# Feed-forward parts of 8 chunks recut to 6, with fewer plain chunks and the operands' steps behind them

## The chip, the cores and the metric

The kernel runs on one core of a Trainium2 chip. The metric is the device time of one execution in microseconds (us), lower is better. TensorE (PE in the profile, its weight loads PEld) multiplies, VectorE (DVE) and GpSimd (POOL) work elementwise, ScalarE (ACT) copies, casts and evaluates functions, SyncE (SP) issues most DMAs.

## The reference

A decoder trunk of two layers on 512 tokens with 1024 features, all in float32. Layer 0 has a causal convolution module, layer 1 differential attention. Behind each comes the same feed-forward and a gated input embedding; the change concerns the feed-forward alone:

```python
D_FF = 2816
def swiglu(x, w_gate, w_up, w_down):
    return (jax.nn.silu(x @ w_gate) * (x @ w_up)) @ w_down
...
u = rms_norm(h, ffn_norm_g[i])
h = h + swiglu(u, ffn_w_gate[i], ffn_w_up[i], ffn_w_down[i])
gate = jax.nn.sigmoid(rms_norm(h, ple_norm_g[i]) @ ple_w_gate[i])
h = h + gate * (p[i] @ ple_w_proj[i])
```

## The kernel before

Features lie on the 128 partitions and tokens along the free axis, so h is eight tiles h[0] to h[7] of 128x512. For accuracy each product of two float32 matrices is three matmuls on rounded operands (`mm3`, L166 to L168): low weight by high input, high by high, high by low. Each weight tile is therefore split into whi (a rounding copy on ScalarE, L159) and wlo (a subtraction on VectorE, L161); the raw tiles have two buffers, whi and wlo four each.

The 2816 hidden features are 22 chunks of 128. They are computed in parts (`PARTS`, pairs of first chunk and count): each part computes its hidden chunks, and a down-projection (`linear`) then adds their share of the result to h. That projection takes eight output tiles m = 0 to 7, the first two of them together, with a weight tile, an accumulator in one of four PSUM banks (mm) and an addition into h on VectorE (L881) for each.

In the first part the chunks are plain. A chunk is a gate and an up product over all eight input tiles, matmuls of 512 columns. The norm's factors are not in the input but come later as rb, since their sum of squares is done beside the first chunk; VectorE multiplies them in (L869, L871), ScalarE applies silu, VectorE multiplies gate by up (L872), and the result is split into high (ScalarE, L874) and low (VectorE, L875) halves, the hidden chunk B0, B1 and so on.

In the other parts two chunks are taken together, and gate and up each become a unit (`Gate`, `Up`) that does the two-by-two block product with seven products in place of eight (a Strassen-like scheme). A product is four groups of three matmuls of 256 columns. For the units the input has to be there as seven combined operands (B11, B21, B22 and T1 to T4), each with high and low parts. `Operands.chunk(k, rb)` makes a quarter of them, for k = 0 to 3, from h and rb: nine instructions on VectorE (L667 twice, L674 to L677, L680, L682, L685) and three on ScalarE (L670, L672, L679), through the temporary tiles B6 and B7, which have one buffer each. These are "the operands' four steps"; `OPS_AT` names the plain chunks behind which they are written down.

The weights of a unit need sums as well: `Unit.prep`, steps 0 to 5, has four sums on POOL (L720, L721, L732, L733), and splits on ScalarE and VectorE (L710, L711; for the first unit of a part L726, L727; L736, L737). `run` interleaves the products of a unit with the preparation of the next one. Products p(4) and p(3) of a unit are done within the next unit; those of a part's last unit come last of all, and its last hidden chunks go through L794, L799, L801 and L802. The first unit of a part is loaded and prepared at m = 5, 6 and 7 of the down-projection ahead of it (`HOOKS`).

The order of instructions on each engine is not the order of the text: a planner places them by the readiness that it simulates, except where an order is written out. So a VectorE instruction can stand ahead of one that the text has earlier.

Of the kernel before, what the change touches and what calls it, by code (L numbers as in the profile page):

```python
# [23 lines left out]
NC = D // P  # L24
# [2 lines left out]
KW = 31  # L27
DFF = 2816
FC = DFF // P
PARTS = [(0, 6), (6, 8), (14, 8)]  # L30
EPS = 1e-6
LAMBDA_INIT = 0.8 - 0.6 * math.exp(-0.3 * 1)
NEG = -1.0e30
# [44 lines left out]
LT = 2  # L78
LA = 4
PACK = True  # L80
OPS_AT = (1, 2, 4, 5)
HOOKS = {5: (None,), 6: (1, 3), 7: (0, 2, 4, 5)}
HT = S // 2
E1 = True
GLO = 1
QKV = (("q", 0, (0, 0, 0, 0)), ("v", 0, (1, 1, 1, 2)), ("q", 1, (1, 1, 1, 2)), ("q", 2, (1, 1, 2, 1)), ("v", 1, (1, 1, 2, 2)), ("q", 3, (1, 1, 1, 1)))

PROJ1 = 16 + 2 + 8 + 2 * FC + 3 * NC + 8 + 4 * len(QKV)


@with_exitstack
def trunk(ctx, tc, xT, pT, wts, diag, dww, vec, rel, onehot, lamv, out):
# [54 lines left out]
    def weight(n=1024, pieces=1, between=(), eng=V, after=(None, None), home=None, parts=None, bufs=1):  # L147
        i = wnext[0]
        wnext[0] += 1
        raw = sb([P, 1024], *(home or ("wraw", 2)))  # L150
        hi = sb([P, 1024], *((parts[0], bufs) if parts else ("whi", 4)), F32R)
        lo = sb([P, 1024], *((parts[1], bufs) if parts else ("wlo", 4)), F32R)
        for k in range(pieces):
            cut = slice(k * n // pieces, (k + 1) * n // pieces)
            loaded[0] = nc.sync.dma_start(raw[:, cut], wts[i, :, cut])
            if k < len(between):
                between[k]()
            with tc.issue_after(after[1].ins) if after[1] else nullcontext():
                A.copy(hi[:, cut], raw[:, cut])  # L159
            with tc.issue_after(after[0].ins) if after[0] else nullcontext():  # L160
                eng.tensor_tensor(lo[:, cut], raw[:, cut], f(hi[:, cut]), ALU.subtract)  # L161
        return hi, lo
# [7 lines left out]
    def weight_in_h(i, c):  # L170

        raw = sb([P, 1024], "wraw", 2)
        nc.sync.dma_start(raw, wts[i])
        parts = [], []
        for k in range(2):
            cut = slice(k * S, (k + 1) * S)
            hi, lo = (sb([P, S], f"h{c + 2 * j + k}", 1, F32R) for j in range(2))
            A.copy(hi, raw[:, cut])
            V.tensor_tensor(lo, raw[:, cut], f(hi), ALU.subtract)
            parts[0].append(hi)  # L180
            parts[1].append(lo)
        return parts
# [622 lines left out]
    def ffn(norm, after, spare):  # L805
# [44 lines left out]
        us = None  # L850
        for at, (f0, n) in enumerate(PARTS):
            if us:
# [4 lines left out]
            for i in range(0 if us else n):  # L857
# [18 lines left out]
                hid.append((hl[:, 0], hl[:, 1]))  # L876
                if i in OPS_AT:
                    ops.chunk(OPS_AT.index(i), rb)

            def add(m, acc):  # L880
                V.tensor_tensor(h[m], acc, h[m], ALU.add)  # L881
                if at == len(PARTS) - 1:
                    after.chunk(m)

            hooks = {}
            if at < len(PARTS) - 1:
                n2 = PARTS[at + 1][1]
                now = wnext[0]
# [146 lines left out]
    def unit_end(pair, tb, q):  # L1035
        t = tp()
        for i in range(4):
            T.transpose(t[:, i * P : (i + 1) * P], q[:, i * P : (i + 1) * P], ident)  # L1038
        t4 = t.rearrange("p (h c t) -> p h c t", h=2, c=2)
        cut = slice(tb * P, (tb + 1) * P)  # L1040
        qs, ks, kl = qk[pair][0:2], qk[pair][2:4], qk[pair][4:6]

        qg, kg = col("q_g"), gains[:, 0:1]
        for c in range(2):
            own, other = HALVES[c], HALVES[1 - c]
            A.activation(qs[c][own, :, cut], t4[own, :, 0], AF.Copy, scale=qg[own])
            A.activation(ks[c][own, :, cut], t4[own, :, 1], AF.Copy, scale=kg[own])
            if KDUP == "A":
                A.activation(ks[c][other, :, cut], t4[own, :, 1], AF.Copy, scale=kg[own])
            else:  # L1050
                G.tensor_copy(ks[c][other, :, cut], f(ks[c][own, :, cut]))
        for c in range(2):
            own, other = HALVES[c], HALVES[1 - c]
            V.scalar_tensor_tensor(
                qs[c][other, :, cut], t4[own, :, 0], qg[own], f(qs[c][own, :, cut]), ALU.mult, ALU.subtract)
            V.scalar_tensor_tensor(
                kl[c][own, :, cut], t4[own, :, 1], kg[own], f(ks[c][own, :, cut]), ALU.mult, ALU.subtract)
# [122 lines left out]
    for what, at, pace in QKV:  # L1180
        ws = slab(GLO if at > 0 else 0)
        for tb in range(4):
# [12 lines left out]
            elif (what, at, tb) == ("q", 0, 2):  # L1195
                n = wnext[0]
                wnext[0] = PROJ1
                pw = [weight(parts=("B6", "B7"))]
# [6 lines left out]
            elif (what, at, tb) == ("q", 2, 1):  # L1205
                pw.append(weight_in_h(PROJ1 + 1, 0))
            elif (what, at, tb) == ("q", 2, 2):
                w_o1 = weight_in_h(PROJ1 + 3, 4)
            elif (what, at, tb) == ("q", 3, 1):
                wnext[0] = PROJ1 + 2  # L1210
                w_o0 = weight(parts=("B0", "B1"))
                wnext[0] = PROJ1 + 4
    unit_end(*waiting)
# [85 lines left out]
def _layout(a):  # L1299
# [12 lines left out]
    def ffn(i):  # L1312
        g, u = _stationary(a["ffn_w_gate"][i]), _stationary(a["ffn_w_up"][i])
        r = []
        for f0, n in PARTS:
            plain = n if f0 == 0 else 0
# [84 lines left out]
```

## Time and profile before

| | us |
|---|---|
| median of 3 runs | 1249.58 (1247.31 to 1250.39) |
| profiled execution | 1249.66 |
| its span, first to last instruction | 1247.6 |
| TensorE busy | 1236.4 |
| VectorE busy | 877.6 |
| ScalarE busy | 623.0 |
| POOL busy | 470.5 |

The granted clock of TensorE was 0.999 over the span. Matmuls overlap in time: each row shows a duration longer than the step from one start to the next, so the step is the pace. In the rows of the profile, tile names stand without buffer numbers: A is the plain input's split tiles (and the units' raw weights and sums), B the hidden chunks and the temporaries B6 and B7, C, wth and bias the combined operands, wraw, whi and wlo the weights, big and wk the work tiles.

### The profile page before, as it was taken

To read this page: it belongs to the slowest core of one execution; us is meant where nothing else is said; L and a number is where in the kernel's file an instruction comes from. 1 tells how busy PE (TensorE), PEld (TensorE's weight loads), DVE (VectorE), ACT (ScalarE), POOL (GpSimd) and SP (SyncE) were. 2 spreads that over 40 slices of the span, in tenths; PEclk is the share of its full clock that TensorE was granted. 3 is DMA by queue.
4 is the path that set the end of the run, shared out by engine and by line. 5 is a ranking of instruction groups with operands and counts; after the bars stand their busy time and mean duration, and the time that the engine had idled before them with its cause. 6 is when DMAs were issued, how large, how long until landed. Compare 5 with 4: busy or idle time off the path is not lost.

```text
span 1247.6 us, 18420 instructions
## 1 busy us (share of the span) xinstructions
PE 1236.4 (99%) x7080; PEld 1081.5 (87%) x7080; DVE 877.6 (70%) x1230; ACT 623.0 (50%) x1096; POOL 470.5 (38%) x355
## 2 busy tenths in 40 slices
PE   9999999999999999999999999999999999999998
PEld 7888788888998899888888888788889998999887
DVE  6998866985895478546676876646966885588535
ACT  5653464533553255334666877735434552455432
POOL 3763442024670365132346635041026640562220
PEclk9999999999999999999999999999999999999999
DMA  7566214324233322334432331142333333233321
GB/s 267 175 205 206 82 51 121 96 97 127 85 102 118 102 87 76 109 104 143 122 119 75 113 92 36 51 147 88 92 118 97 102 117 108 82 102 88 104 97 67
DMA packets 49154, 136.33 MB, mean 109 GB/s; under 512 B 5635, under 2 KB 10243, under 8 KB 49068
## 3 DMA queue, kind: packets, MB, share of 16 engines
q1 hardware_dynamic: 46944, 131.74, 33.7%
q10 hardware_dynamic: 2124, 3.43, 1.0%
q8 instruction: 55, 0.90, 0.3%
q14 instruction: 31, 0.25, 0.1%
HBM read 128.84 MB, written 6.31 MB: 108 GB/s over the span
## 4 chain that ended last, share of the span: by engine, by line
PE 88%; DVE 5%; issue 2%; DMA 1%; ACT 1%; SPq 0%; POOL 0%; DVEq 0%; ACTq 0%
PE mm L166 27%; PE mm L167 27%; PE mm L168 27%; PE mm L1117 1%; DVE sc L449 1%; DVE wlo L161 1%; PE sc L1085 1%; PE sc L1084 1%; PE tp L1104 1%; PE sc L398 1%; PE mm L398 1%; PE tp L1038 1%; PE mm L354 1%; PE tp L199 1%; DVE wlo L711 0%
## 5 line engine op out<-in xcount | busy, mean ns | idle before, releaser
L159 ACT CAST whi<-wraw 128x1024 fp32r<-128x1024 f32 (+2 forms) x145 | 145.6, 1013 | 220.2 <-PE mm L168 97.2
L161 DVE TENSOR_TENSOR wlo<-wraw,whi 128x1024 fp32r<-128x1024 f32 (+2 forms) x141 | 179.3, 1277 | 73.7 <-ACT whi L159 73.5
L166 PE MATMUL mm<-A,wlo 128*128 128x512 f32 (+1 forms) x568 | 222.5, 392 | 0.3 <-ACT A L206 0.2
L167 PE MATMUL mm<-A,whi 128*128 128x512 f32 (+1 forms) x568 | 219.8, 388 | 0.0
L168 PE MATMUL mm<-A,whi 128*128 128x512 f32 (+1 forms) x568 | 217.6, 389 | 0.0
L166 PE MATMUL mm<-B,wlo 128*128 128x512 f32 x352 | 137.9, 392 | 0.0
L167 PE MATMUL mm<-B,whi 128*128 128x512 f32 x352 | 137.8, 391 | 0.0
L168 PE MATMUL mm<-B,whi 128*128 128x512 f32 x352 | 136.2, 391 | 0.0
L229 POOL TENSOR_TENSOR acc<-acc,wk 128x512 f32<-128x512 f32 x35 | 58.3, 1665 | 194.5 <-ACT wk L228 193.9
L166 PEld LDWEIGHTS mm<-A,wlo 128*128 128x128 f32 x568 | 106.9, 188 | 23.6 <-issue 1.4
L167 PE MATMUL mm<-C,whi 128*128 128x256 f32 x448 | 127.0, 283 | 0.0
L168 PE MATMUL mm<-C,whi 128*128 128x256 f32 x448 | 127.0, 283 | 0.0
L166 PE MATMUL mm<-C,wlo 128*128 128x256 f32 x448 | 127.0, 283 | 0.0
L167 PEld LDWEIGHTS mm<-A,whi 128*128 128x128 f32 x568 | 107.0, 188 | 22.0 <-issue 1.0
L168 PEld LDWEIGHTS mm<-A,whi 128*128 128x128 f32 x568 | 106.6, 188 | 21.9 <-issue 0.5
L711 DVE TENSOR_TENSOR wlo<-A,whi 128x1024 fp32r<-128x1024 f32 x60 | 104.6, 1752 | 21.0 <-ACT whi L710 21.0
L710 ACT CAST whi<-A 128x1024 fp32r<-128x1024 f32 x60 | 62.9, 1048 | 56.6 <-PE mm L168 45.3
L720 POOL TENSOR_TENSOR A<-wraw 128x512 f32<-128x512 f32 x16 | 25.4, 1589 | 170.3 <-DMA wraw<-in_wts 156.1
L720 POOL TENSOR_TENSOR A<-A 128x512 f32<-128x512 f32 x16 | 25.3, 1581 | 161.9 <-DMA A<-in_wts 159.2
L167 PEld LDWEIGHTS mm<-C,whi 128*128 128x128 f32 x448 | 86.1, 192 | 0.2
L166 PEld LDWEIGHTS mm<-C,wlo 128*128 128x128 f32 x448 | 86.1, 192 | 0.2
L168 PEld LDWEIGHTS mm<-C,whi 128*128 128x128 f32 x448 | 86.1, 192 | 0.0
(309 smaller groups left out, 3030.6 us busy)
## 6 DMA issues: line engine op xcount, KB each, us to landing
wraw<-in_wts SPq DMA_DIRECT2D x161, 512.0 KB, 3.6
A<-in_wts SPq DMA_DIRECT2D x32, 512.0 KB, 3.6
wraw<-in_wts SPq DMA_DIRECT2D x16, 384.0 KB, 3.1
D<-in_diag SPq DMA_DIRECT2D x22, 256.0 KB, 4.7
C<-in_diag SPq DMA_DIRECT2D x16, 256.0 KB, 4.4
h<-in_xT SPq DMA_DIRECT2D x8, 256.0 KB, 5.2
rest<-h SPq DMA_DIRECT2D x8, 256.0 KB, 2.5
bias<-scr ACTq DMA_DIRECT2D x8, 256.0 KB, 3.7
```

Source lines behind the costliest of these rows:

```text
L159: A.copy(hi[:, cut], raw[:, cut])
L161: eng.tensor_tensor(lo[:, cut], raw[:, cut], f(hi[:, cut]), ALU.subtract)
L166: T.matmul(acc, al, bh, start=first, stop=False, **kw)
L167: T.matmul(acc, ah, bh, start=False, stop=False, **kw)
L168: return T.matmul(acc, ah, bl, start=False, stop=last, **kw)
L199: r = T.matmul(t[:, cut], src[:, cut], ones, start=first and b == 0, stop=last and b == 3)
L229: self.last = self.eng.tensor_tensor(self.acc, self.acc, sq, ALU.add)
L354: last_tap[0] = T.matmul(acc, dg[:, j % 4], ups[c][:, j : j + S], start=(j == 0), stop=(j == PE_TAPS[c] - 1))
L398: last_tap[0] = T.matmul(acc[:, g * P : (g + 1) * P], w, ups[c][:, g, LEAD - m : LEAD - m + P], start=(m == 0), stop=(m == LAGS - 1),)
L710: A.copy(hi, src)
L711: V.tensor_tensor(lo, src, f(hi), ALU.subtract)
L720: G.tensor_tensor(s[:, 0], r1[:, 0], r1[:, 1], ALU.add)
```

## The change

Three constants and a count:

```diff
-PARTS = [(0, 6), (6, 8), (14, 8)]
+PARTS = [(0, 4), (4, 6), (10, 6), (16, 6)]
...
-OPS_AT = (1, 2, 4, 5)
+OPS_AT = (0, 1, 2, 3)
...
-PROJ1 = 16 + 2 + 8 + 2 * FC + 3 * NC + 8 + 4 * len(QKV)
+PROJ1 = 16 + 2 + 8 + 2 * FC + len(PARTS) * NC + 8 + 4 * len(QKV)
```

In each layer the first part has four plain chunks instead of six. The other 18 chunks, 16 before, are seven-product chunks in three parts of six, before two parts of eight. There is one down-projection more per layer; the four have 4, 6, 6 and 6 chunks as input, the three had 6, 8 and 8. The operands' four steps are written behind plain chunks 0, 1, 2 and 3. `PROJ1` is the index of a later weight tile in the packed array, which shifts with the number of down-projection tiles. The host packs the same weights in the new order.

## The prediction

> **What bounds the kernel now.** I read the page first (busy times, then the chain that ended last), then the busy time of the engines in stretches of the first layer's feed-forward, then the order of time of TensorE and of VectorE at its seams. From the page:
>
> ```profile
> span 1247.6 us, 18420 instructions
> ...
> PE 1236.4 (99%) x7080; PEld 1081.5 (87%) x7080; DVE 877.6 (70%) x1230; ACT 623.0 (50%) x1096; POOL 470.5 (38%) x355
> ...
> PE 88%; DVE 5%; issue 2%; DMA 1%; ACT 1%; SPq 0%; POOL 0%; DVEq 0%; ACTq 0%
> ```
>
> TensorE (PE) has 11 us of idle time in the whole span and makes 88% of the chain. So what counts is how many matmuls there are, and whether the change makes TensorE wait. The pace, with matmuls pipelined, is read from start to start:
>
> ```profile
> 225.44 0.39 PE L168 MATMUL mm<-A,whi 128*128 128x512 f32 x1
> ...
> 245.84 0.39 PE L168 MATMUL mm<-A,whi 128*128 128x512 f32 x1
> ...
> 301.62 0.39 PE L168 MATMUL mm<-B,whi 128*128 128x512 f32 x1
> 301.85 0.28 PE L166 MATMUL mm<-wth,wlo 128*128 128x256 f32 x1
> ...
> 324.12 0.28 PE L166 MATMUL mm<-C,wlo 128*128 128x256 f32 x1
> ```
>
> In the plain chunks the groups of three (L166, L167, L168) repeat every 0.68 us: 30 groups lie between 225.44 and 245.84, so a 128x512 matmul takes 20.40 / 90 = 0.2267 us. In the seven-product units a group takes 0.36 us: 62 groups from 301.85 to 324.12, so a 128x256 matmul takes 22.27 / 186 = 0.1197 us. The seam from the first down-projection to the seven-product units (301.62 to 301.85) is one ordinary step of 0.23 us: a seam costs TensorE nothing as long as the next operands are there. The other engines decide that. The columns are the stretch and its length, then PE, PEld, DVE, ACT and POOL busy with their instruction counts, granted clock, DMA:
>
> ```profile
> 220.00:247.00 27.00, 27.00 (x121) 22.35 (x120) 26.27 (x42) 14.12 (x21) 0.00 (x0) 1.00 0.28 83
> 247.00:269.00 22.00, 22.00 (x99) 18.23 (x98) 15.64 (x24) 8.75 (x12) 0.00 (x0) 1.00 0.36 118
> 269.00:302.00 33.00, 33.00 (x148) 27.34 (x147) 22.02 (x22) 10.20 (x13) 12.25 (x8) 1.00 0.37 111
> 302.00:382.00 80.00, 79.64 (x657) 79.11 (x656) 65.02 (x67) 42.89 (x75) 48.90 (x28) 1.00 0.33 100
> 388.00:427.00 39.00, 39.00 (x171) 31.92 (x171) 18.34 (x21) 9.98 (x11) 9.86 (x7) 1.00 0.35 107
> 427.00:505.00 78.00, 78.00 (x652) 77.91 (x651) 60.16 (x66) 43.79 (x75) 37.67 (x22) 1.00 0.27 83
> 948.00:1026.00 78.00, 77.85 (x649) 77.61 (x648) 64.28 (x67) 42.82 (x74) 51.31 (x28) 1.00 0.32 97
> ```
>
> The first two rows are the plain chunks after their factors (rb) arrive, the third the first down-projection, then units (first run), the second down-projection, units (second run), and the first run of layer 2. VectorE (DVE) is full from 220 to 247, where the operands' steps run, has 6.4 us to spare in the next 22 us and 11.0 us in the first down-projection. TensorE loses 0.36 us and 0.15 us in the first runs of the two layers, nothing in the second run.
>
> **The change, part by part.** *Two chunks per layer go from plain to seven products.* Plain, two chunks are 2 x 2 x 8 x 3 = 96 wide matmuls: 96 x 0.2267 = 21.76 us. As a gate and an up unit they are 2 x 7 x 4 x 3 = 168 half-wide ones: 168 x 0.1197 = 20.11 us. Gain 1.65 us per layer, 3.3 us in all. The down-projection's matmuls stay: 22 chunks x 8 x 3 per layer however the parts are cut.
>
> The Trainium skill (TensorE: Matmul & The Clock Gate, "Wait — 56ns, not 53.3ns?") gives N / 2.4 GHz + about 2.5 ns per warm matmul, by which I estimate 215.8 and 109.2 ns, so a gain of 20.72 - 18.35 = 2.37 us per layer and 4.7 us in all. The rows above show a larger fixed part, which the half-wide form pays twice as often; they are used.
>
> *One part more per layer.* A fourth down-projection adds eight loads, eight splits of weights (which are narrower, 512 and 768 columns for 768 and 1024, so their columns in all stay the same) and eight additions into h (L881). VectorE gets 8 x 0.69 = 5.5 us for these additions, in stretches where 39 us hold 18.34 us of its work: free. Bound: nothing to 0.25 us per seam, by the step at 301.62; I take nothing. SP's queue carries the same bytes in eight more issues per layer.
>
> *The operands' four steps move up,* from behind chunks 1, 2, 4, 5 to behind chunks 0 to 3. Each is nine VectorE instructions (L667 twice, L674 to L677, L680, L682, L685) and three on ScalarE, with no DMA and nothing on POOL. None can start before rb at 220, and the first already starts there, so the move gains nothing at the front. What changes is the end: the plain stage now stops after four chunks, 21.8 us earlier, at about 247, where VectorE is full. Groups of VectorE between 219 and 269:
>
> ```profile
> L161 DVE TENSOR_TENSOR wlo<-wraw,whi 128x1024 fp32r<-128x1024 f32 x6 | 7.3, 1221 | 0.0
> L667 DVE SCALAR_TENSOR_TENSOR B<-h,vec,rb 128x512 f32<-128x512 f32 x8 | 5.6, 748 | 0.1
> L685 DVE TENSOR_TENSOR C<-B,C 128x1024 fp32r<-128x1024 f32 x4 | 4.9, 1217 | 0.0
> ...
> L682 DVE TENSOR_TENSOR C<-B,C 128x512 fp32r<-128x512 f32 x3 | 2.1, 684 | 0.0
> L677 DVE TENSOR_TENSOR B<-B,B 128x256 f32<-128x256 f32 x4 | 1.7, 422 | 0.0
> ```
>
> A step is 2 x 0.70 + 5 x 0.42 + 0.68 + 1.22 = 5.4 us, four 21.6. From 220 to 269 VectorE will have: four steps 21.6; four plain chunks at four 512-wide instructions (0.69), 11.0; two plain splits 2.4; eight down splits, 512 wide, 5.5; eight additions 5.5; the first unit's operands (three 512-wide, three 1024-wide) 5.7. Sum 51.7 us in 49 us. Today the same kinds of work have 82 us, from 220 to 302. On top comes POOL, whose four sums for a unit fall now at about 247, where today they fall at 270:
>
> ```profile
> 269.87 1.29 POOL L720 TENSOR_TENSOR A<-A 128x512 f32<-128x512 f32 x1 [56.62 <-DMA A<-in_wts]
> ...
> 274.90 1.62 POOL L733 TENSOR_TENSOR A<-A,A 128x512 f32<-128x512 f32 x1
> ```
> ```profile
> 260.78 1.22 DVE L685 TENSOR_TENSOR C<-B,C 128x1024 fp32r<-128x1024 f32 x1
> ...
> 270.19 1.53 DVE L872 TENSOR_TENSOR big<-big,big 128x512 f32<-128x512 f32 x1
> 271.64 2.04 DVE L161 TENSOR_TENSOR wlo<-wraw,whi 128x768 fp32r<-128x768 f32 x1
> 273.60 1.77 DVE L727 TENSOR_TENSOR wk<-A,wk 128x512 fp32r<-128x512 f32 x1
> 275.30 1.77 DVE L875 TENSOR_TENSOR B<-big,B 128x512 fp32r<-128x512 f32 x1
> ```
>
> In POOL's 6.65 us VectorE takes 7.1 us for four instructions that elsewhere take 0.69 (three) and about 0.92 (three quarters of a 1024-wide 1.22), so some 4.1 us are lost; two units' sums fall into the stage: 8 us. VectorE comes out of the stage about 51.7 + 8 - 49 = 10.7 us behind.
>
> The Trainium skill (SBUF — State Buffer, "SBUF: two separate sides") says why: VectorE instructions with two SBUF inputs and GpSimd share a port pair under an exclusive lock, and the loser blocks for the whole instruction. The rows agree in kind. By the rule VectorE could lose as much as POOL is busy, 2 x 6.65 = 13.3 us, and be 16 us behind.
>
> What of this lies on TensorE's path? Not the backlog itself, only what is needed at once. (a) The last plain chunk's hidden half (L875): at 247 TensorE has 18 wide matmuls of two accumulators that need only chunks 0 to 2, then four on the new high half; today L875 ends at 277.1, 8.1 us after its stage. 22 matmuls are 5.0 us, and a third accumulator's nine make 7.0: short by 0 to 3.1 us. (b) Weights for m=4 to 7: an accumulator takes 12 x 0.2267 = 2.72 us now, and they are prepared three ahead. (c) The first unit's A11 and the last step's operands: wanted at 269; the last step ends at 262.0 today (the L685 above); some 7 us less work lies ahead of it then (a plain chunk's 2.75, four splits at 1.22, less the down splits) and POOL's 4 us more, so about 259, 10 us ahead of need. (d) The backlog then goes into the first run, where 80 us of units leave VectorE 15 us, so 60 us leave about 11: just enough. So the price per layer lies between nothing and 10.7 us (all of it waited for). I take 0.6 us, near the low end, because the nearest row, today's seam at 269, has the same late L875 and no gap.
>
> *The tails.* At the end of a run two products of the last up unit (p(4), p(3)) come after the others, and the down-projection's first matmuls fill the waits:
>
> ```profile
> 380.18 0.40 PE L166 MATMUL mm<-B,wlo 128*128 128x512 f32 x1
> ...
> 384.74 0.39 PE L168 MATMUL mm<-B,whi 128*128 128x512 f32 x1
> 384.96 0.28 PE L166 MATMUL mm<-C,wlo 128*128 128x256 f32 x1
> ```
> ```profile
> 390.51 0.68 DVE L802 TENSOR_TENSOR B<-wk,B 128x512 fp32r<-128x512 f32 x1
> ```
>
> 21 fill matmuls, the 24 products to 387.8, and the last hidden half at 391.2, 3.4 us later. With eight chunks in a part, 36 matmuls need neither of the last two chunks; with six, 24 do. After 21 of them 3 are left (0.7 us), and a third accumulator's 12 (2.7 us), whose bank comes free when L794 has read it: 3.4 us against 3.4. Cost nothing if the order takes the third accumulator, 2.7 us per tail if not, with six tails instead of four.
>
> Sum: 1249.66 (the profiled execution, span 1247.6) - 3.3 + 2 x 0.6 = 1247.6 us. The profiled execution is 0.08 us above the median of 1249.58.
>
> **The rivals.** *Clean gain:* no new wait, and the shorter first runs no longer let VectorE fall behind, so today's 0.5 us goes too: 1249.66 - 3.3 - 0.5 = 1245.9 us. For it: TensorE's second run shows no loss at all. Against: VectorE enters the first run late instead of early.
>
> *The matmul's fixed cost is what the page has:* a saving of 4.7 us, 1244.9 us. The paces above speak against it; they are measured in the same stages.
>
> *VectorE's backlog reaches TensorE (slower):* the stage from 220 to 269 is overbooked, and what VectorE serves late is L875, the weights of m=4 to 7, or the last step. It decides once VectorE is more than about 5 us behind where a matmul waits. At two thirds of the 10.7 us, 7 us per layer: 1246.4 + 14 = 1260 us. If half of that, 1253.4.
>
> *Tails without cover (slower):* 2.7 us at six tails, 1246.4 + 16 = 1262.6 us; decided by whether the third accumulator's matmuls stand ahead of the late ones on TensorE. For it: the 21 fill matmuls are used up before p(4) today.
>
> **How the numbers follow.** Within 0.3% is 1245.8 to 1253.3 around the median, about what a measurement of this kernel can tell from no change. My forecast (small gain less small waits, 1245.9 to 1250) has 0.52; the clean gain 0.23, most of which lies on the bound itself; the page's pace 0.02; the backlog 0.14; the tails 0.09. Of the clean gain and the pace 0.2 in all come out faster; of the two slower rivals about 0.2 end above 1253.3, the rest is the same. The range goes from the page's pace to a backlog of which somewhat more than half is waited for, 1244.9 to 1255, and leaves out about 0.18: the far ends of the slower rivals and a gain beyond the rule.
>
> **What the profile would show.** Right: 96 fewer wide and 168 more half-wide matmuls per layer; first plain stage 43.5 us after its start instead of 65.3; VectorE full from 220 to 269 and some 10 us behind in the first unit; no TensorE gap above 1 us at the new seams. Wrong: idle time of TensorE before L168 released by L875, or before L166 by L161 (backlog); gaps of 2 to 3 us after p(3) (tails); VectorE idle in the first down-projection, which would mean the overbooking is miscounted.

## The result and the profile after

| | before | after |
|---|---|---|
| median of 5 runs, us | 1249.58 (1247.31 to 1250.39) | 1261.05 (1260.51 to 1263.03) |
| profiled execution, us | 1249.66 | 1263.03 |
| its span, us | 1247.6 | 1261.0 |
| granted clock over the span | 0.999 | 0.995 |

The ratio after to before is 1.0095, 95% interval 1.0085 to 1.0106: slower by 11.5 us. It lies above the predicted range. The profiled execution is the slowest of the five, 2.0 us above their median.

The page of the changed kernel:

```profile
span 1261.0 us, 18890 instructions
...
PE 1238.4 (98%) x7224; PEld 1087.2 (86%) x7224; DVE 903.3 (72%) x1278; ACT 638.9 (51%) x1138; POOL 498.3 (40%) x371
...
PE 85%; DVE 6%; DMA 2%; issue 1%; ACT 0%; POOL 0%; SPq 0%; DVEq 0%; ACTq 0%; POOLq 0%
```

TensorE has 144 matmuls more (72 per layer: 168 half-wide in, 96 wide out), as it should. Its idle time has doubled from 11 to 23 us, and VectorE's share of the chain has grown. The view of TensorE's waits of the changed kernel (us in total, times, longest) names two lines that were no wait before (a wait is written as the waiting instruction, `<-`, and what released it):

```profile
PE mm L166 <- DVE wlo L161: 7.5, 2, 3.7
PE mm L168 <- DVE B L875: 2.5, 2, 1.6
```

Both come once per layer. TensorE's order of time shows where: the first down-projection, which begins at 248.4.

```profile
258.15 0.39 PE L167 MATMUL mm<-B,whi 128*128 128x512 f32 x1
260.10 1.20 PE L168 MATMUL mm<-B,whi 128*128 128x512 f32 x4 [1.56 <-DVE B L875]
265.03 0.80 PE L166 MATMUL mm<-B,wlo 128*128 128x512 f32 x1 [3.73 <-DVE wlo L161]
265.63 0.63 PE L167 MATMUL mm<-B,whi 128*128 128x512 f32 x1
266.05 0.63 PE L168 MATMUL mm<-B,whi 128*128 128x512 f32 x1
...
270.75 0.49 PE L167 MATMUL mm<-B,whi 128*128 128x512 f32 x1
...
278.82 0.28 PE L166 MATMUL mm<-wth,wlo 128*128 128x256 f32 x1
```

From 265.63 to 266.05 a step is 0.42 us where it should be 0.227. The stretches show why, in the columns of the prediction's table (the last but two is the granted clock); the last two rows are the same place in the second layer (here, as in the expectations, the layers are counted 1 and 2):

```profile
220.00:247.00 27.00, 27.00 (x119) 22.14 (x118) 25.33 (x44) 13.22 (x21) 0.00 (x0) 1.00 0.22 72
248.40:265.00 16.60, 11.34 (x49) 8.74 (x47) 16.50 (x22) 5.95 (x10) 6.70 (x4) 0.97 0.11 34
265.00:270.70 5.70, 5.67 (x13) 4.47 (x14) 2.10 (x4) 1.38 (x3) 0.00 (x0) 0.50 0.43 111
270.70:278.80 8.10, 8.10 (x36) 6.67 (x35) 6.56 (x6) 3.64 (x4) 4.26 (x3) 0.98 0.68 205
900.70:917.00 16.30, 11.68 (x49) 8.68 (x48) 16.19 (x22) 6.02 (x10) 6.59 (x4) 0.97 0.09 25
917.00:922.70 5.70, 5.62 (x13) 4.45 (x14) 2.11 (x5) 1.34 (x3) 0.00 (x0) 0.50 0.41 110
```

VectorE is full until TensorE stands, TensorE stands for 3.7 us, and then works for 5.7 us at half its clock. The first down-projection takes 30.4 us in layer 1 (248.41 to 278.82) and 30.1 us in layer 2 (900.75 to 930.82), where 96 matmuls at 0.2267 are 21.8. Of the 8.6 and 8.3 us beyond that, the wait for the low half (L875) is about 1.7 and 1.1, counted from start to start less an ordinary step, the wait for the weights of m=4 (L161) 3.9 and 3.9, the half clock 2.9 and 2.8; 0.1 and 0.5 are left in small steps.

The feed-forwards are counted here from the matmuls behind the norm's sums (219.10 before, 220.08 after) to the end of the last down-projection. Apart from the first down-projection they are 5.1 us shorter than before: 3.3 us as foreseen, about 1 us of stalls that the old first runs had (78.3 and 78.1 us against 77.7 in the second runs) and the remainder in steps of a few hundredths. So the feed-forwards are 16.9 - 5.1 = 11.8 us longer (338.4 and 338.3 us against 332.6 and 332.3). The 13.4 us between the spans hold 1.6 us more from outside them; the medians, 11.5 us apart, do not.

VectorE's order of time in the changed kernel, around the first wait, and POOL's:

```profile
248.61 0.69 DVE L871 TENSOR_TENSOR big<-mm,rb 128x512 f32<-128x512 f32 x1
249.21 1.22 DVE L685 TENSOR_TENSOR C<-B,C 128x1024 fp32r<-128x1024 f32 x1
250.34 1.78 DVE L161 TENSOR_TENSOR wlo<-wraw,whi 128x512 fp32r<-128x512 f32 x1
252.05 1.52 DVE L680 TENSOR_TENSOR bias<-B,bias 128x256 fp32r<-128x256 f32 x1
253.49 1.77 DVE L872 TENSOR_TENSOR big<-big,big 128x512 f32<-128x512 f32 x1
255.19 1.78 DVE L727 TENSOR_TENSOR wk<-A,wk 128x512 fp32r<-128x512 f32 x1
256.89 0.68 DVE L682 TENSOR_TENSOR C<-B,C 128x512 fp32r<-128x512 f32 x1
...
259.37 0.68 DVE L875 TENSOR_TENSOR B<-big,B 128x512 fp32r<-128x512 f32 x1
...
260.76 1.28 DVE L881 TENSOR_TENSOR h<-mm,h 128x512 f32<-128x512 f32 x2
261.95 1.22 DVE L685 TENSOR_TENSOR C<-B,C 128x1024 fp32r<-128x1024 f32 x1
263.09 1.28 DVE L881 TENSOR_TENSOR h<-mm,h 128x512 f32<-128x512 f32 x2
264.29 1.28 DVE L161 TENSOR_TENSOR wlo<-wraw,whi 128x512 fp32r<-128x512 f32 x2
```
```profile
249.64 1.94 POOL L720 TENSOR_TENSOR A<-A 128x512 f32<-128x512 f32 x1 [35.41 <-DMA A<-in_wts]
...
254.80 1.62 POOL L733 TENSOR_TENSOR A<-A,A 128x512 f32<-128x512 f32 x1
```

The chain reads so. After the plain stage VectorE still has the last two operands' steps (L667 to L685), the first unit's operands (L727, L737) and weight splits to do. POOL's four sums fall into the same 6.8 us and stretch VectorE's instructions (L680 takes 0.42 without them, in run 2 below). So the last chunk's L872 comes late, and its low half, L875, ends at 260.0. By 258.4 TensorE has done all that needs no low half: 44 matmuls of four accumulators. Four of one kind are left, and all four accumulators end together at about 261. So all four banks and all four pairs of weight tiles come free only now, and m=4's copy on ScalarE and split on VectorE come late, and other work stands ahead of both: on ScalarE a step's cast (L679, the copy starts at 261.8), on VectorE two double additions and a step's last sum. The first of the two splits ends at about 265.0, and TensorE goes on.

### The profile page after: what moved, and what is told of

Its sections match the earlier page's. It is cut to its first block, busy times and chain, and to the rows that moved or that the text cites. A ratio compares the mean times of both kernels' runs of the same rounds, so it can differ in the third digit from the quotient of the medians.

```text
span 1261.0 us, 18890 instructions
## 1 busy us (share of the span) xinstructions
PE 1238.4 (98%) x7224; PEld 1087.2 (86%) x7224; DVE 903.3 (72%) x1278; ACT 638.9 (51%) x1138; POOL 498.3 (40%) x371
## 4 chain that ended last, share of the span: by engine, by line
PE 85%; DVE 6%; DMA 2%; issue 1%; ACT 0%; POOL 0%; SPq 0%; DVEq 0%; ACTq 0%; POOLq 0%
PE mm L166 26%; PE mm L167 26%; PE mm L168 26%; PE mm L1117 1%; DVE wlo L161 1%; DMA wraw<-in_wts 1%; DVE sc L449 1%; PE sc L1085 1%; PE sc L1084 1%; PE tp L1104 1%; PE sc L398 1%; PE mm L398 1%; DVE h L881 1%; PE tp L1038 1%; PE mm L354 1%
## 5 line engine op out<-in xcount | busy, mean ns | idle before, releaser
L161 DVE TENSOR_TENSOR wlo<-wraw,whi 128x1024 fp32r<-128x1024 f32 (+2 forms) x149 | 175.7, 1183 | 78.7 <-ACT whi L159 78.7
L166 PE MATMUL mm<-A,wlo 128*128 128x512 f32 (+1 forms) x504 | 197.1, 391 | 1.8 <-ACT A L206 1.6
L167 PE MATMUL mm<-A,whi 128*128 128x512 f32 (+1 forms) x504 | 194.4, 387 | 0.0
L168 PE MATMUL mm<-A,whi 128*128 128x512 f32 (+1 forms) x504 | 192.4, 389 | 0.0
L166 PE MATMUL mm<-B,wlo 128*128 128x512 f32 x352 | 140.7, 400 | 7.5 <-DVE wlo L161 7.5
L168 PE MATMUL mm<-C,whi 128*128 128x256 f32 x492 | 139.2, 283 | 0.0
L167 PE MATMUL mm<-C,whi 128*128 128x256 f32 x492 | 139.2, 283 | 0.0
L166 PE MATMUL mm<-C,wlo 128*128 128x256 f32 x492 | 139.2, 283 | 0.0
L168 PE MATMUL mm<-B,whi 128*128 128x512 f32 x352 | 135.3, 395 | 2.5 <-DVE B L875 2.5
L711 DVE TENSOR_TENSOR wlo<-A,whi 128x1024 fp32r<-128x1024 f32 x66 | 113.7, 1729 | 23.9 <-ACT whi L710 23.9
L166 PEld LDWEIGHTS mm<-A,wlo 128*128 128x128 f32 x504 | 94.7, 188 | 23.2 <-ACT A L206 2.6
L167 PEld LDWEIGHTS mm<-A,whi 128*128 128x128 f32 x504 | 94.7, 188 | 19.5 <-issue 1.0
L168 PEld LDWEIGHTS mm<-A,whi 128*128 128x128 f32 x504 | 94.5, 188 | 19.5 <-issue 0.5
L167 PEld LDWEIGHTS mm<-C,whi 128*128 128x128 f32 x492 | 94.4, 192 | 0.2
L166 PEld LDWEIGHTS mm<-C,wlo 128*128 128x128 f32 x492 | 94.4, 192 | 0.2
L168 PEld LDWEIGHTS mm<-C,whi 128*128 128x128 f32 x492 | 94.4, 192 | 0.0
L166 PEld LDWEIGHTS mm<-B,wlo 128*128 128x128 f32 x352 | 67.5, 192 | 24.0 <-DVE wlo L161 9.9
```

The lines of the kernel that those rows point to most:

```text
L166: T.matmul(acc, al, bh, start=first, stop=False, **kw)
L167: T.matmul(acc, ah, bh, start=False, stop=False, **kw)
L168: return T.matmul(acc, ah, bl, start=False, stop=last, **kw)
L711: V.tensor_tensor(lo, src, f(hi), ALU.subtract)
```

## The experiments

Each kernel was compared with the kernel before on the same chip. Edits are against the changed kernel unless said otherwise. Theory A: the late low half ties the accumulators and weight tiles, and the rest follows. Theory B: VectorE has too much work in this stage, in whatever order. Theories C and D are stated in the expectations in which they first appear.

**1. The low half first.** The operands' step behind the last plain chunk, and the first unit's preparation likewise, may not be issued before the last low half.

```diff
-ops.chunk(OPS_AT.index(i), rb)
+with tc.issue_after(low.ins) if i == n - 1 else nullcontext():   # low: the last L875
+    ops.chunk(OPS_AT.index(i), rb)
```

> Same products and parts as the changed kernel; on VectorE alone the last operands' step and the first unit's splits are queued behind the last plain chunk's low half (L875). Theory A (that half comes late, so four accumulators end together, their four weight tiles stay taken, the next two weights come late and the idle time halves TensorE's clock): L875 ends near 252 instead of 260, all three losses go (2.8 us of waits for L875, 7.8 us for the weights, 5.7 us of slow clock, over both layers): 1261.0 - 16.3 = about 1245, at most 1248. Theory B (VectorE is overbooked in the stage whatever the order, so the wait only moves to the weights or the first unit): above 1255.

Measured 1259.49 us, ratio 1.0081 (1.0064 to 1.0098). The wait for the low half is gone, but TensorE's waits have this in its place:

```profile
PE mm L166 <- DVE wlo L161: 9.3, 2, 4.8
```

In VectorE's order of time of this kernel L875 ends at 256.1, and then what was held back comes (L882 is L881):

```profile
254.34 1.77 DVE L875 TENSOR_TENSOR B<-big,B 128x512 fp32r<-128x512 f32 x1
256.03 1.40 DVE L667 SCALAR_TENSOR_TENSOR B<-h,vec,rb 128x512 f32<-128x512 f32 x2
...
261.11 1.87 DVE L882 TENSOR_TENSOR h<-mm,h 128x512 f32<-128x512 f32 x3
262.90 0.67 DVE L161 TENSOR_TENSOR wlo<-wraw,whi 128x512 fp32r<-128x512 f32 x1
```

This order alone moves the wait, and saves 1.6 us of medians. That speaks for B, though here too the split that TensorE waits for (262.90) stands behind three additions and 5.1 us of the work held back.

**2. POOL's sums later.** The first unit's load waits behind the weight load of m=5 on SP's queue, so that POOL's sums come at 257 to 263 instead of 250 to 256.

```diff
+with tc.issue_after(loaded[0].ins) if at == 0 and k is None else nullcontext():
     x.load() if k is None else x.prep(k)
```

> The changed kernel, but the first unit's two weight loads stand behind the weight load of m=5 on SP's queue, so that POOL's four sums come some 5 us later and no longer beside VectorE's work ahead of L875; TensorE's order is the same. Theory A: without POOL beside it and without the first unit's splits ahead of it L875 ends near 254, TensorE does not wait for it, and four weight tiles come free near 259.3; the wait for the next weights shrinks from 3.9 to about 2.5 us and is too short to halve the clock: 1261.0 - 2.8 - 2.8 - 5.7 = about 1250. Theory B: POOL then slows the weights' splits instead, the gap ahead of m=4 stays at 3.9 us or more with the half clock: 1256 to 1261.

Measured 1256.99 us, ratio 1.0064 (1.0049 to 1.0079): 4.1 us saved. VectorE's order of time in this kernel:

```profile
251.15 0.42 DVE L680 TENSOR_TENSOR bias<-B,bias 128x256 fp32r<-128x256 f32 x1
251.49 0.68 DVE L872 TENSOR_TENSOR big<-big,big 128x512 f32<-128x512 f32 x1
...
253.36 0.68 DVE L875 TENSOR_TENSOR B<-big,B 128x512 fp32r<-128x512 f32 x1
...
259.01 1.89 DVE L881 TENSOR_TENSOR h<-mm,h 128x512 f32<-128x512 f32 x3 [1.83 <-PE mm L168]
260.81 0.68 DVE L727 TENSOR_TENSOR wk<-A,wk 128x512 fp32r<-128x512 f32 x1
261.41 0.68 DVE L881 TENSOR_TENSOR h<-mm,h 128x512 f32<-128x512 f32 x1
262.01 1.75 DVE L161 TENSOR_TENSOR wlo<-wraw,whi 128x512 fp32r<-128x512 f32 x2
```

L875 ends at 254.0 instead of 260.0. Two things changed ahead of it: every instruction has its undisturbed duration (four of them took 4.4 us longer before), and three of the first unit's preparation (L727 twice, L737, 1.8 us) now come behind it. Yet TensorE keeps its order, with the four matmuls on the low half last (at 258.58), so the four accumulators still end together. VectorE even stands idle for 1.8 us until they do, and TensorE then waits 3.6 and 4.0 us for m=4. Of the 3.6 us, ScalarE's copy of m=4 takes until 259.7, and VectorE comes to its split at 262.0, behind four additions, three of which came together, and an L727. Here it is the tie and the order behind it, not VectorE's amount of work, that make the wait: a point for A, although the time, the wait and the half clock behind it are those expected under B. POOL beside the splits, B's account of them, lengthens them by some 0.5 us only.

**3. Own tiles for the weights of m=4 and 5,** so that they need not wait for an accumulator to end.

```diff
-linear(n, hid, add, 2, at=hooks)
+linear(n, hid, add, 2, at=hooks, own={4: "B4", 5: "B5"} if at == 0 else {})
```

> The changed kernel, with tiles of their own for the weights of m=4 and m=5 of the first down-projection (B4 and B5, unused there), so that they need not wait for a tile of m=0 or m=1. Theory A: the wait for L875 stays (about 1.4 us per layer), the 3.9 us wait and the half clock go: 1261.0 - 7.8 - 5.7 = about 1247.5. Theory B: VectorE is still behind, and a wait of 2 us or more comes at m=6 or at the first unit: above 1253.

Measured 1253.94 us, ratio 1.0034 (1.0021 to 1.0047): 7.1 us saved, the most of the edits that keep the recut and compute everything, but not the 13.5 us that theory A expected. TensorE's waits of this kernel (its lines are 10 further down: L178 is L168, L176 is L166, L886 is L875, L892 is L881):

```profile
PE mm L178 <- DVE B L886: 3.9, 2, 2.2
...
PE mm L176 <- DVE h L892: 1.4, 2, 0.7
```

The wait for weights is gone, and with it the slow clock in layer 2; in layer 1 it still lasts 3.4 us. The first down-projection takes 26.8 and 24.7 us instead of 30.4 and 30.1, and the run of units behind it 57.5 and 58.1: with the work unchanged and in the old order, most of the loss does not come back there. That is against B in its strict form. What remains is the late low half and a bank that an addition has not yet freed.

**4. and 5. Matmuls to fill the wait.** 20, then 8 matmuls with ones into a spare bank between m=3 and m=4. They change no result.

```diff
+if m == 4 and keep_busy:
+    for _ in range(20):        # 8 in the second
+        last_of[0] = T.matmul(d[:, :HT], ones, f(src[0][0])[:, :HT], start=True, stop=True)
```

> The changed kernel with 20 idle matmuls (ones by a hidden half, 256 columns, some 0.22 us each by the step of the 512-wide ones-matmuls of 0.43 us) put on TensorE between m=3 and m=4 of the first down-projection; their result is not used. All waits stay. Theory A with the clock as its third part: the stretch at half clock goes, 5.7 us less, and the filler is some 0.5 us per layer longer than the wait: about 1256. If the slow stretch had another cause than the idle time: 1261 to 1262.

> The changed kernel with 8 idle matmuls in place of 20 between m=3 and m=4 (in the profile of the longer filler 20 made 40 pieces in 8.4 us, so 8 take about 3.4 us and fit into the 3.9 us wait). If the idle time is what halves the clock afterwards: no stretch below full clock, 2 x 2.9 us less than the changed kernel, 1255.5. If the slow stretch has another cause: 1261.

Twenty: 1267.05 us, ratio 1.0144 (1.0129 to 1.0159). Eight: 1260.02 us, ratio 1.0087 (1.0072 to 1.0102). Neither has a slow stretch: the granted clock over the span is 1.0 in both. So it is the idle time that brings the clock down. Twenty took twice the time that had been estimated, since each is recorded as two pieces of 0.21 us (40 in 8.8 us), longer than the wait that they fill. With eight the first down-projection takes 27.6 and 27.5 us instead of 30.4 and 30.1. But the first runs of units behind it take 59.0 and 59.7 us instead of 57.5: they now wait for VectorE and ScalarE, so of the 5.4 us only 1.0 arrives in the median.

**6. and 7. Work moved behind the critical place.** The fourth step is put behind the second addition, and the first unit's preparation behind it; then the same with the own tiles of 3.

```diff
-if i in OPS_AT:
+if i in OPS_AT[:3]:
...
+if at == 0 and m == 1:
+    with tc.issue_after(added[0].ins):    # added: the last L881
+        ops.chunk(3, rb)
```

> The changed kernel with the fourth operands' step, and the first unit's splits on VectorE, moved behind the second addition into h (L881 at m=1) of the first down-projection. Nothing is left out. Theory C (VectorE is some 10 us behind, TensorE has cover for four accumulators only, and then stands still until VectorE, in its fixed order, has served the low half, the additions that free the banks and the next weights): what TensorE needs now stands ahead of 9 us of work that it needs only at the units, so the low half ends near 252 to 256, the weights of m=4 come in time, no half clock: 1261.0 - 16.3 = about 1245, at most 1248. Theory B (overbooked in sum): the same time is lost at the start of the units, where the fourth step's operands are late: 1253 or more.

> As the kernel with the fourth step behind m=1, and with tiles of their own for the weights of m=4 and m=5. Theory C: if the order alone suffices this adds nothing (within 1 us of that kernel, about 1245); if a weight tile is still waited for there, up to 3 us better. Theory B: 1253 or more in both.

1261.03 us, ratio 1.0091 (1.0077 to 1.0105), and 1259.04 us, ratio 1.0071 (1.0058 to 1.0083). TensorE's waits of the first of the two:

```profile
PE mm L166 <- DVE wlo L711: 7.2, 2, 4.2
PE mm L166 <- DVE wlo L161: 3.3, 2, 1.6
```

and of the second (L722 is L711):

```profile
PE mm L176 <- DVE wlo L722: 8.6, 3, 4.7
```

The first down-projection shrinks to 23.7 us, but now the first run of units stands for 4.2 us at L711, which splits the first unit's weights, again with a stretch at half clock behind it. That run takes 63.4 us instead of 57.5 in layer 1. With own tiles no wait is left in the down-projection at all, and the time is still 9.6 us above before. The wait follows the work, as B has it; theory C's 1245 us did not come. But POOL is beside the work again. The row of VectorE that TensorE waits for in run 6:

```profile
275.78 2.28 DVE L711 TENSOR_TENSOR wlo<-wraw,whi 128x1024 fp32r<-128x1024 f32 x1
```

Undisturbed L711 takes 1.22 us (at 269.03 in the same run). With the three instructions ahead of it (L727, L737, another L711) VectorE loses 4.3 us beside POOL's sums in this place, as much as TensorE waits. So these two runs do not tell VectorE's own excess from what POOL takes of it.

**8. One step less.** The fourth step is left out and the third's operands stand in for its own (part of the result is therefore not computed).

```diff
+if k < 3: ops.chunk(k, rb)
+else:
+    for n_ in ops.at: ops.at[n_][3] = ops.at[n_][2]
```

> The changed kernel without the fourth operands' step; the units take the third step's operands in its place (so a quarter of the input is left out). VectorE has 5.4 us per layer less to do in the stage. Theory C: the waits go with that work, because the weights and additions then stand earlier on VectorE: no wait above 1 us, no half clock, about 1245 to 1248. If only the tie to four weight tiles mattered, and not the amount of work: the wait at m=4 stays above 3 us, 1255 or more.

1251.62 us, ratio 1.0015 (1.0006 to 1.0024): 5.4 us less of VectorE's work per layer give 9.4 us in all, where theory C expected 13 to 16. There is no slow stretch, and the waits for L161 are 2.2 us in total. The first down-projection takes 23.3 and 23.0 us; 4.1 us of this gain are lost again in the first runs of units (59.2 and 59.9 us instead of 57.5). A step has three casts on ScalarE too, but ScalarE was busy for 5.95 of the 16.6 us from 248.4, so it was not the one short of time. No slow clock follows the waits that are left, and so 10.8 us less work on an engine that was not the busiest give nearly as much in time.

**9. Only one step,** the other three left out in the same way: is there any other cause in this place, such as late DMAs?

> The changed kernel with the first operands' step alone; the units take its operands for all four quarters (three quarters of the input are left out). VectorE has 16.2 us per layer less to do in the first stage, far less than it can serve. Theory B (VectorE overbooked) alone: no wait is left in the first down-projection, 1244.8 within 1. Theory D (a down-projection of four chunks has also a feed too slow for 2.72 us per weight: two raw tiles, a load of some 3 us, a copy and a split): waits of 1 to 3 us per layer remain for the weights of m=4 to m=7, 1247 to 1251.

1248.51 us, ratio 0.9994 (0.9985 to 1.0004). Its stretches:

```profile
220.00:247.00 27.00, 27.00 (x120) 22.34 (x119) 17.16 (x27) 10.02 (x15) 0.00 (x0) 1.00 0.24 80
247.00:270.00 23.00, 23.00 (x106) 18.91 (x105) 17.46 (x21) 8.36 (x12) 8.29 (x6) 1.00 0.39 131
```

VectorE has slack in both, TensorE none, and the first down-projection takes 22.0 us. Its banks, weight tiles and loads are as in the changed kernel, so these alone do not make the loss. The time is one that theory D had named, but the waits that it expected did not come. The recut still gains little with VectorE out of the way: the feed-forwards are 1.2 us shorter than before (331.9 and 331.8 us), since the first runs take 59.3 us instead of 57.5: TensorE now waits there, twice in each, for ScalarE's copies of products (L760, L765).

**10. The parts alone, at the other end.** Six plain chunks first as before, and the four-chunk part last:

```diff
-PARTS = [(0, 4), (4, 6), (10, 6), (16, 6)]
+PARTS = [(0, 6), (6, 6), (12, 6), (18, 4)]
-OPS_AT = (0, 1, 2, 3)
+OPS_AT = (1, 2, 4, 5)
```

> Parts of 6 plain, then 6, 6 and 4 seven-product chunks, steps behind chunks 1, 2, 4, 5 as in the kernel before: a fourth down-projection without fewer plain chunks. All theories and the prediction: the added seam and the tails of six and four chunks cost next to nothing, 1249.5 within 1.5 us. If tails with less cover cost 2.7 us at two more places per layer or more: 1255 or more.

1254.61 us, ratio 1.004 (1.0026 to 1.0054). This has one down-projection more, the plain stage of before, and is slower nevertheless, where 1249.5 us was expected. TensorE's waits of this kernel, ScalarE's row ahead of the first of them, and TensorE's row at the second:

```profile
PE mm L166 <- DVE wlo L161: 5.9, 4, 1.7
```
```profile
542.85 0.62 ACT L159 CAST whi<-wraw 128x512 fp32r<-128x512 f32 x1 [0.82 <-DMA wraw<-in_wts]
```
```profile
554.06 0.50 PE L166 MATMUL mm<-A,wlo 128*128 128x512 f32 x1 [1.68 <-DVE wlo L161]
```

In each layer one wait lies in the last down-projection, of four chunks, and one at the first matmul behind it, whose weights come through the same two raw tiles. In that down-projection an accumulator takes 12 x 0.2267 = 2.7 us. Two loads were issued at 539.3; the first landed at 542.8, and after copy and split the tiles were free for the next loads, issued at 546.6 and 549.0: some 3.7 us per weight tile. The split of the first (545.05) also stood behind VectorE's work for the next norm.

**11. The same with raw tiles of their own** for m = 4 to 7 of that down-projection (B6 and B7, free by then). The edit is against the kernel of 10.

```diff
-linear(n, hid, add, 2, at=hooks)
+linear(n, hid, add, 2, at=hooks, own=own if at == 3 else None)   # own: raw tiles in B6, B7
```

> Parts 6, 6, 6 and 4 as before, but in the last down-projection the raw weights of m=4 to 7 lie in tiles of their own (B6, B7), so that their loads need not wait for the two raw tiles. Theory D: the waits for the splits there (1.6 and 1.8 us in layer 1, 1.3 and 1.8 in layer 2) go, 1254.6 - 6 = about 1249. If VectorE's and ScalarE's work for the next norm is what makes the splits late: 1253 or more.

1248.21 us, ratio 0.9988 (0.9979 to 0.9998): 6.4 us less than 10, and L161 is no longer among TensorE's waits. So in this place the two raw tiles were the limit; the work for the next norm stayed. It is the fastest version that computes everything, 0.12% under the kernel before, with an interval that only just leaves out no change, and its plain stage is the one of before.

**12. The operands' steps alone:** the kernel before with `OPS_AT = (0, 1, 2, 3)`.

> The kernel before with the operands' steps written behind chunks 0 to 3 and nothing else changed. All theories: 1249.5 within 1.5 us, since the first step starts when the factors arrive in either case and two chunks more follow the last step.

1248.99 us, ratio 0.9999 (0.9989 to 1.0008): with six plain chunks their place costs nothing. What costs is that the stage in which they are done is 21.8 us shorter.

## Why the prediction was wrong

- *The step that failed* is the price of VectorE's backlog. The prediction counted VectorE as 10.7 us behind, bounded the price per layer by nothing and 10.7 us, and took 0.6 us, "because the nearest row, today's seam at 269, has the same late L875 and no gap". Measured were 8.6 and 8.3 us, of which 5.6 and 5.0 are waits and the rest, nearly all, the half clock. The old seam was the wrong row to go by. It has L875 late, but VectorE has 11 us to spare behind it and each of the down-projection's accumulators is 18 matmuls long, not 12. The rival "VectorE's backlog reaches TensorE", 1260 us at 0.14, is what came, at the two lines that the prediction had named for it. That its number fits as well is partly luck: its 14 us were waits alone, where 10.6 us of waits and 5.7 us of slow clock came.
- *That VectorE is full was right* (25.3 of 27 us from 220, then 16.5 of 16.6), though not the whole count: two units' POOL sums were put into the stage at 8 us, and one unit's came, at 4.4 us; the next begins at 274.5. Runs 8 and 9 show that without this work there is no such loss: 5.4 us less per layer saves 9.4 us in all, 16 us less takes the waits in the down-projection away.
- *(a), the low half, short by 0 to 3.1 us,* held in the number only: 1.7 and 1.1 us. By its own terms it was 1.1 to 3.1 (8.1 less 7.0 or 5.0). L875 ended 11.6 us after the plain stage in layer 1, not 8.1, and TensorE had 10.0 us of work without it, not 5.0 to 7.0. The two errors cancel; that is luck.
- *(b), the weights of m=4 to 7, "prepared three ahead",* was given no price and cost 3.9 us per layer. Three ahead does not help when the four tiles are held by four accumulators that all lack the same low half. Run 3 shows the size of it, 7.1 us with the clock, of 11.5; run 2 shows that the tie acts even when the low half itself is early, as long as TensorE's order has it last.
- *The half clock* was in no term and no rival: 2.9 and 2.8 us.
- *(c), the last step's operands,* came later than forecast (263.2, not about 259), but TensorE did not wait for them.
- *(d), a backlog that goes into the first run,* "just enough", was not free. The changed kernel shows no stall there, after TensorE had already waited in the down-projection. Where that wait was filled or moved (runs 5, 6, 7), the first run stalled instead.
- *The gain of 3.3 us* held, as far as it can be seen: the plain stage is 21.8 us shorter (43.5 us), a run of units in a part of six takes 57.5 us, which is 480 matmuls at 0.1197, and run 9 has hardly any loss in the down-projection (22.0 us against 21.8). No run that computes everything shows the gain in its time. Run 11, 1.7 us shorter than before in its two feed-forwards (331.6 us each), does not bear on it, since it has six plain chunks.
- *An extra part costs nothing* was right for parts of six (no gap at their seams) and no rule: with four chunks in the last down-projection weights are late there and behind it, and run 10 is 5.2 us slower than the kernel before.
- *The tails cost nothing* was right at all six. TensorE's order of time in the changed kernel at the first of them:

```profile
340.89 0.39 PE L168 MATMUL mm<-B,whi 128*128 128x512 f32 x1
341.12 0.28 PE L166 MATMUL mm<-C,wlo 128*128 128x256 f32 x1
...
343.87 0.28 PE L168 MATMUL mm<-C,whi 128*128 128x256 f32 x1
343.99 0.40 PE L166 MATMUL mm<-B,wlo 128*128 128x512 f32 x1
```

Every step is an ordinary one; the matmuls of further accumulators stand ahead of the late products.

What stays open is how the loss divides between VectorE's load and the tied tiles: the work taken away in run 8 saves 9.4 us and the tiles of run 3 save 7.1 us, so the two overlap. How much of VectorE's load is POOL's doing was not measured by itself either. The recut of the change with both the own tiles and the later POOL sums of run 2 was not tried.

## What to carry to other kernels

Shortening the matmuls of a stage raises the load of every other engine in that stage. Where one is near full, the matrix engine waits for its excess unless there are tiles enough to run on without it; moving the work behind the critical place only moved the wait here. An excess in the first stage behind which slack follows is covered only as far as TensorE can run on without it, and that is set by the accumulators and weight tiles (here four, 44 matmuls, 10 us), which a late operand that all need holds together. Price such a wait with what comes behind it, the clock too, and look for the row with the same load and the same length, not only the same instruction.

## What the runs showed of the hardware

After a wait of 3.7 us, with 0.9 us of work and another wait of 1.6 us ahead of it, TensorE's granted clock was 0.50 for 5.7 us and then 0.98 and more. It was so in both layers. The half clock also came behind the single waits of 4.5 and 4.8 us in run 1 (for 4.4 and 5.7 us), of 3.6 and 4.0 us in run 2 (for about 3 us, in layer 1 three matmuls late), of 4.2 and 3.1 us in run 6 (for 3.3 and 6.2 us) and of 3.7 and 4.7 us in run 7 (for 5.1 and 5.9 us). In run 3 it came in layer 1, after waits of 2.2 and 0.7 us with 0.9 us of work between them, and not in layer 2, after 1.7 and 0.7 us. After the 1.6 us waits in run 6 and the waits of 1.2 us and less in run 8 it did not come, and with the ones matmuls in the gap (runs 4 and 5) never. The Trainium skill (TensorE: Matmul & The Clock Gate, "What's actually happening") has half rate after an idle window of about 3.4 us. The single waits agree but for the 3.1 us in run 6, which is a little shorter, and in layer 1 of run 3 no single wait was as long.

Beside POOL's sums VectorE's instructions with two inputs took 1.5 to 1.8 us where they take 0.4 to 0.7 otherwise (256 and 512 columns). The prediction knew the stretch, and its 4.1 us for one unit's sums held (4.4 us in the changed kernel). Run 2, without it ahead of L875 and with three of the first unit's instructions moved as well, has L875 6.0 us earlier (254.0 against 260.0) and is 4.1 us of medians faster. A matmul of ones by a hidden half, both read as plain float32, 256 columns, was recorded as two pieces of 0.21 us, against one with a step of 0.12 for the kernel's rounded operands.
